# One rotating pool of eight PSUM banks instead of two pools of four, in a transformer forward pass on one core

## The chip, the cores and the metric

The kernel runs on one core of one Trainium2 chip. The metric is the device time of one execution in microseconds. Five engines work beside each other, each in its own order: TensorE (PE: matmuls, and the weight loads, PEld), VectorE (DVE), ScalarE (ACT), GpSimd (POOL) and SyncE (SP), which issues nearly all loads and stores. PE writes its results into PSUM, a memory of eight banks; a bank takes 128 partitions by 512 fp32 numbers. DVE and ACT read results out of it.

## What is computed

A batch of one, 1024 tokens of width 1024, fp32, through two blocks of two layers each. The first block's layers take one wide projection of the normalised input and feed two mixers beside each other; the second block has one gMLP layer and one chunk-attention layer.

```python
for layer in range(DEPTH):                      # first block, twice
    proj = rms_norm(x, norm_w[layer]) @ w_in[layer]
    (q, k, v, z_attn, q_h, f_h, i_h, g_h, gate_attn, gate_hgrn) = jnp.split(proj, split_points, axis=-1)
    q, k = partial_rope(q), partial_rope(k)     # 8 heads of 64, 2 key heads
    a = sliding_window_attention(q, k, v, attn_sinks[layer]) * jax.nn.silu(z_attn)
    b = norm(hgrn2_recurrence(q_h, k_h, i_h, logf)) * jax.nn.silu(g_h)
    merged = sigmoid(gate_attn) * (a @ w_up_attn[layer]) + sigmoid(gate_hgrn) * (b @ w_up_hgrn[layer])
    x = x + merged @ w_out[layer]
x = rms_norm(x, final_norm_w)
# second block
u, v, z = jnp.split(rms_norm_2(x, a_norm_g) @ a_w_in, 3, axis=-1)
x = x + (gelu(u) * (w_s @ layer_norm(gelu(v)) + b_s) * silu(z)) @ a_w_out
k, v = jnp.split(rms_norm_2(x, g_kv) @ w_kv, 2, axis=-1)
q, z = jnp.split(rms_norm_2(x, b_norm_g) @ w_qz, 2, axis=-1)
o = softmax(q @ k.T + rel_bias, over the own and the 8 earlier chunks of 64) @ v
x = x + (o * silu(z)) @ w_out
out = rms_norm_2(x, final_norm_g)
```

## The kernel before

**Products.** Every large product is done in about fp32 precision by three matmuls: each operand is split into a high and a low float32r part, and hi·hi, hi·lo and lo·hi are added in one PSUM bank. Weights come from DRAM as raw tiles of 128x1024 (fetch_w, L218 issues the load on SP), are split by a cast (ACT or DVE) and a subtraction (DVE or POOL) into wh and wl, and are used by one of three loops: unit (L259 to L261, output channels by 512 tokens), unit_tok (L272 to L274, tokens by 256 channels) and unit_wide (L286 to L288, tokens by 512 channels, two banks at once). The bank that such a product adds up in comes from Net.mm (L143); the 512 tokens of a half, or a quarter of them at the very start, are handled as a whole. All elementwise work goes through Engine.call, so that all of it is recorded at L77 whatever it does; the trace tells such instructions apart by their tiles (hp are tiles of the common heap).

**Everything else that PE does** takes its bank from Net.aux (L146): the sums of squares over the channels (a matmul with a matrix of ones: load_first L1143 at the start, mean_bcast L363 for the norms, out_last L1007 at the end), the transposes and scores of the sliding attention (swa_kv_fiber L553 for the keys, whose split is in tiles khl; swa_q_fiber L594 for the queries, L614 for the scores, L642 and L667 behind the softmax), the recurrence (hgrn_half L683 to L800), the gMLP's bias (gmlp_bias: L1214 sums, ACT copies the sum, L1219 spreads it; L1274 mixes) and the chunk attention (attn2's block: scores L1413 into aux, DVE adds the bias and reduces to the maximum in one instruction, which writes the scores to sP and the maximum to a2m; exp on ACT, scaling on POOL; transposes L1446 into aux, copied to pT; products with the values L1456).

**half_banks** (L149) gives the two heads of a block (e = 0 and e = 1) the two 256-column halves of one aux bank where their scores, or their transposes, are no wider than 256 columns; otherwise each takes a bank.

**The order of the work** is set in two steps. The program issues units of weights one after the other, and between them, each time that 24 matmuls' worth of product work has passed (tick), advances the open fibers (the attention's and the recurrence's steps, the norms' late parts) by one step. Behind that a scheduler writes each engine's order, from the dependences and from when it reckons that an instruction's operands and its bank are free. In the kernel before, a tile from mm waits for the fourth product tile ahead of it to be read out, and a tile from aux for the fourth aux tile ahead of it.

Of the kernel before, what the change touches and what calls it, by code (L numbers as in the profile page):

```python
# [9 lines left out]
F32 = mybir.dt.float32  # L10
# [9 lines left out]
P = 128  # L20
H = 512
# [76 lines left out]
class Net:  # L98
# [42 lines left out]
        return self.heap(F32R), self.heap(F32R)  # L141

    def mm(self):  # L143
        return self.ps.tile([P, H], F32, tag="mm", bufs=4, name=self.name("mm"))

    def aux(self):  # L146
        return self.ps.tile([P, H], F32, tag="aux", bufs=4, name=self.name("aux"))

    def half_banks(self):  # L149

# [1550 lines left out]
```

## Time and profile before

| | |
|---|---|
| time of three runs | 3031.61, 3034.82, 3035.86 us (median 3034.82) |
| the profiled execution's own time | 3037.59 us |
| its span in the trace | 3035.8 us |
| mean granted clock of TensorE | 0.990 |
| busy PE, PEld | 2944.6, 2444.6 us |
| busy DVE, ACT, POOL | 1767.0, 1472.9, 1162.0 us |
| matmuls and other PE instructions | 15996 |

The span is the stretch from the first to the last instruction of the profiled execution; what of its own time lies outside is 1.8 us. Busy time counts the time in which an engine executes something. The idle time before an instruction is put down to the engine and tile whose end released it; the tiles' names are those of the program with their numbers left out.

### The profile page before, as it was taken

The numbers are of one execution on the slowest core, as the hardware profiler recorded it, in microseconds if no ns is written. First come the engines' busy times: TensorE is split into PE (matmuls) and PEld (weight loads), VectorE is DVE, ScalarE is ACT, GpSimd is POOL, SyncE is SP. The second block draws the span as 40 slices with busy tenths as digits, with TensorE's granted clock in tenths as the row PEclk, the third lists the DMA queues.
The fourth block names the chain that finished last, engine by engine and source line by source line (L and its number), as shares of the span: only waits on it lengthen the run. The fifth ranks groups of instructions, "written<-read, shape, count | busy, mean of one in ns | idle before, by whom it ended". The sixth has DMA issues, their size and how long they took to land.

```text
span 3035.8 us, 43390 instructions
## 1 busy us (share of the span) xinstructions
PE 2944.6 (97%) x15996; PEld 2444.6 (81%) x15996; DVE 1767.0 (58%) x3376; ACT 1472.9 (49%) x2966; POOL 1162.0 (38%) x1217
## 2 busy tenths in 40 slices
PE   6999999999999999999999999999998999999997
PEld 6887888888878888788878888888887787878777
DVE  6557755566665666665666434454345655555566
ACT  4665336642366424674244554335544546455552
POOL 4445433543435434454332333223333434333331
PEclk9999999999999999999999999999999999999999
DMA  3212242122521224322243223433243101111123
GB/s 119 78 63 101 87 139 84 68 73 90 174 84 63 77 91 139 109 72 70 91 139 125 104 100 123 133 115 116 104 146 105 58 31 54 45 54 38 62 102 108
DMA packets 101493, 283.44 MB, mean 93 GB/s; under 512 B 11289, under 2 KB 15513, under 8 KB 101281
## 3 DMA queue, kind: packets, MB, share of 16 engines
q1 hardware_dynamic: 100016, 279.51, 27.0%
q8 instruction: 126, 2.06, 0.3%
q10 hardware_dynamic: 1264, 1.17, 0.1%
q14 instruction: 87, 0.70, 0.1%
HBM read 259.66 MB, written 20.97 MB: 92 GB/s over the span
## 4 chain that ended last, share of the span: by engine, by line
PE 86%; DVE 7%; issue 2%; ACT 2%; POOL 1%; DMA 1%; SPq 0%; DVEq 0%; POOLq 0%; ACTq 0%
PE mm L259 20%; PE mm L260 20%; PE mm L261 19%; DVE hp L77 5%; PE mm L288 3%; PE mm L286 3%; PE mm L287 3%; PE aux L683 2%; PE aux L1413 2%; PE aux L1456 1%; PE aux L1446 1%; PE mm L273 1%; PE mm L274 1%; PE mm L272 1%; PE aux L614 1%
## 5 line engine op out<-in xcount | busy, mean ns | idle before, releaser
L259 PE MATMUL mm<-hp,wh 128*128 128x512 f32 (+1 forms) x2816 | 1107.8, 393 | 1.9 <-DVE hp L77 1.9
L260 PE MATMUL mm<-hp,wh 128*128 128x512 f32 (+1 forms) x2816 | 1095.6, 389 | 0.5 <-POOL hp L77 0.5
L261 PE MATMUL mm<-hp,wl 128*128 128x512 f32 (+1 forms) x2816 | 1095.0, 389 | 0.0
L77 POOL TENSOR_TENSOR wl<-raw,wh 128x512 fp32r<-128x512 f32 x381 | 513.5, 1350 | 771.7 <-ACT wh L77 667.2
L77 POOL TENSOR_TENSOR hp<-hp,hp 128x256 f32<-128x256 f32 (+4 forms) x378 | 430.3, 1143 | 688.9 <-DVE hp L77 270.6
L77 ACT CAST wh<-raw 128x512 fp32r<-128x512 f32 x569 | 350.8, 620 | 676.8 <-PE mm L260 464.8
L259 PEld LDWEIGHTS mm<-hp,wh 128*128 128x128 f32 x2816 | 532.0, 189 | 108.1 <-issue 3.1
L261 PEld LDWEIGHTS mm<-hp,wl 128*128 128x128 f32 x2816 | 531.8, 189 | 108.3
L260 PEld LDWEIGHTS mm<-hp,wh 128*128 128x128 f32 x2816 | 532.6, 189 | 105.5 <-issue 2.6
L77 DVE TENSOR_TENSOR wl<-raw,wh 128x512 fp32r<-128x512 f32 x435 | 356.6, 822 | 215.1 <-ACT wh L77 172.8
L77 DVE TENSOR_TENSOR hp<-hp,hp 128x512 fp32r<-128x512 f32 (+3 forms) x472 | 368.3, 788 | 157.8 <-ACT hp L77 110.7
L77 ACT ACT_TABLE_LOAD x244 | 313.1, 1283 | 34.4 <-PE mm L261 15.4
L77 ACT CAST hp<-hp 128x512 fp32r<-128x512 f32 (+2 forms) x254 | 146.0, 583 | 233.8 <-POOL hp L77 183.9
L77 DVE CAST wh<-raw 128x512 fp32r<-128x512 f32 x247 | 132.3, 536 | 194.9 <-PE mm L260 165.0
L77 ACT ACTIVATE hp<-mm 128x512 f32<-128x512 f32 (+1 forms) x304 | 171.1, 574 | 152.6 <-PE mm L288 74.8
L77 DVE TENSOR_TENSOR hp<-mm,hp 128x512 f32<-128x512 f32 (+1 forms) x248 | 155.3, 633 | 144.6 <-ACT hp L77 58.8
L286 PE MATMUL mm<-wh,hp 128*128 128x512 f32 x480 | 188.2, 392 | 0.0
L287 PE MATMUL mm<-wl,hp 128*128 128x512 f32 x480 | 187.5, 391 | 0.0
L288 PE MATMUL mm<-wh,hp 128*128 128x512 f32 x480 | 187.3, 390 | 0.0
L77 POOL TENSOR_SCALAR sP<-sP,a2l 128x640 f32<-128x640 f32 (+4 forms) x128 | 88.8, 698 | 230.3 <-DVE a2l L77 181.6
L272 PE MATMUL mm<-wh,hp 128*128 128x256 f32 x448 | 129.5, 289 | 7.2 <-ACT hp L77 7.2
L77 ACT ACTIVATE sP<-sP,a2nm 128x640 f32<-128x640 f32 (+4 forms) x128 | 88.4, 691 | 96.8 <-DVE a2nm L77 95.7
(183 smaller groups left out, 3472.9 us busy)
## 6 DMA issues: line engine op xcount, KB each, us to landing
raw<-in_w_ch_dram SPq DMA_DIRECT2D x128, 512.0 KB, 3.3
raw<-in_g_uz_dram SPq DMA_DIRECT2D x64, 512.0 KB, 3.2
hp<-xd SPq DMA_DIRECT2D x88, 256.0 KB, 4.3
raw<-in_w_up_dram SPq DMA_DIRECT2D x64, 256.0 KB, 2.7
raw<-in_w_o_dram SPq DMA_DIRECT2D x32, 512.0 KB, 3.3
raw<-in_g_v_dram SPq DMA_DIRECT2D x32, 512.0 KB, 4.3
raw<-in_g_o_dram SPq DMA_DIRECT2D x32, 512.0 KB, 3.8
raw<-in_w_wide_dram SPq DMA_DIRECT2D x28, 512.0 KB, 4.0
```

The lines of the kernel that those rows point to most:

```text
L77: self.last = f(*args, **kw)
L259: nc.tensor.matmul(ps, wh[:, c : c + P], rh, start=(k == 0), stop=False)
L260: nc.tensor.matmul(ps, wh[:, c : c + P], rl, start=False, stop=False)
L261: nc.tensor.matmul(ps, wl[:, c : c + P], rh, start=False, stop=(k == nk - 1))
L272: nc.tensor.matmul(ps, lh[:, o : o + P], wh[:, c : c + n], start=(k == 0), stop=False)
L273: nc.tensor.matmul(ps, lh[:, o : o + P], wl[:, c : c + n], start=False, stop=False)
L274: nc.tensor.matmul(ps, ll[:, o : o + P], wh[:, c : c + n], start=False, stop=(k == KD - 1))
L286: nc.tensor.matmul(ps, lh[:, s], wh, start=(k == 0), stop=False)
L287: nc.tensor.matmul(ps, lh[:, s], wl, start=False, stop=False)
L288: nc.tensor.matmul(ps, ll[:, s], wh, start=False, stop=(k == KD - 1))
L683: nc.tensor.matmul(ps[:, s], k[:, s], q[:, s], start=True, stop=True)
L1413: nc.tensor.matmul(ps[:, 0:w], st[p, kk][e][half][:, o : o + P], st[p, "k"][e][hf][:, k0 : k0 + w], start=(j == 0), stop=(j == 1),)
```

## The change

The two helpers that hand out PSUM banks name one tag instead of two, so that all eight banks form one rotation:

```diff
--- before.py
+++ after.py
@@ -141,10 +141,10 @@
         return self.heap(F32R), self.heap(F32R)
 
     def mm(self):
-        return self.ps.tile([P, H], F32, tag="mm", bufs=4, name=self.name("mm"))
+        return self.ps.tile([P, H], F32, tag="bank", bufs=8, name=self.name("mm"))
 
     def aux(self):
-        return self.ps.tile([P, H], F32, tag="aux", bufs=4, name=self.name("aux"))
+        return self.ps.tile([P, H], F32, tag="bank", bufs=8, name=self.name("aux"))
 
     def half_banks(self):
```

A tile of either kind now waits for the eighth tile ahead of it, of whichever kind, to be read out. Nothing else in the program text changes; the same instructions are issued on every engine. The scheduler, which reckons with the new waits, writes another order: it differs on PE in some 800 rows, on DVE and ACT in some 250 each, on POOL in 71 and on SP in 20. In the rows below, a name's last number counts the program's tiles; + and - stand for the order now and before.

PE, from its first instructions on (L1143 sums squares of a quarter of the input; mm_299, mm_332 and mm_359 are the first products; 49 of their matmuls lie between the first and the last row):

```order
 L1143 MATMUL aux18_132<-hp14_121,ones_f_91 128x256 x2
+L1143 MATMUL aux49_209<-hp45_198,ones_f_91 128x256 x2
 L272 MATMUL mm92_299<-wh21_142,hp29_159 128x256
 L273 MATMUL mm92_299<-wl22_143,hp29_159 128x256
...
 L274 MATMUL mm99_332<-wh27_154,hp44_195 128x256
 L272 MATMUL mm100_359<-wh53_221,hp29_159 128x256
-L1143 MATMUL aux49_209<-hp45_198,ones_f_91 128x256 x2
 L273 MATMUL mm100_359<-wl54_222,hp29_159 128x256
```

The second quarter's squares moved from behind 49 matmuls to ahead of them.

PE at the norm behind the first half of the first block's second layer (L363 sums squares; mm2368 and mm2376 are products of 128x256 for the second half's tokens):

```order
 L274 MATMUL mm2368_11270<-wh2311_11111,hp2289_11014 128x256
+L363 MATMUL aux2369_11297<-hp2317_11149,ones_d_83 128x512
 L272 MATMUL mm2376_11319<-wh2304_11097,hp2241_10834 128x256
...
 L274 MATMUL mm2376_11319<-wh2311_11111,hp2287_11009 128x256
-L363 MATMUL aux2369_11297<-hp2317_11149,ones_d_83 128x512
 L272 MATMUL mm2376_11319<-wh2311_11111,hp2288_11013 128x256
```

The sum now stands straight behind mm2368, ahead of 21 matmuls of mm2376 that it stood behind.

PE in the chunk attention (scores L1413 of a block into aux4424, transposes L1446 of an earlier block, mm4436 a product):

```order
 L1446 MATMUL aux4417_21350<-ident_76,sP4375_21160 128x128
-L259 MATMUL mm4436_21413<-hp4105_19829,wh4337_20948 128x512
 L1413 MATMUL aux4424_21372<-hp4231_20521,hp4295_20810 128x256
 L1413 MATMUL aux4424_21372<-hp4231_20521,hp4296_20811 128x256
...
 L1413 MATMUL aux4429_21388<-hp4320_20901,hp4297_20816 128x512
 L1413 MATMUL aux4429_21388<-hp4320_20901,hp4298_20817 128x512
+L259 MATMUL mm4436_21413<-hp4105_19829,wh4337_20948 128x512
 L260 MATMUL mm4436_21413<-hp4106_19830,wh4337_20948 128x512
```

One product that stood ahead of a block's scores now stands behind the first of them; the second half of that bank comes after it as before.

## Rows read from the trace of the kernel before

**Rows 1.** The page: totals by engine, and the chain that ended last by engine.

```profile
PE 2944.6 (97%) x15996; PEld 2444.6 (81%) x15996; DVE 1767.0 (58%) x3376; ACT 1472.9 (49%) x2966; POOL 1162.0 (38%) x1217
...
PE 86%; DVE 7%; issue 2%; ACT 2%; POOL 1%; DMA 1%; SPq 0%; DVEq 0%; POOLq 0%; ACTq 0%
```

**Rows 2.** Busy time by stretch: its length, engines' busy us (instructions), granted clock, DMA.

```profile
2280.00:2356.00 76.00, 66.11 (x329) 56.65 (x329) 45.62 (x71) 40.10 (x98) 29.70 (x22) 0.93 0.29 102
2356.00:2432.00 76.00, 69.37 (x445) 56.79 (x443) 51.22 (x129) 42.44 (x116) 35.85 (x38) 0.98 0.17 56
```

**Rows 3.** What PE waited for over the span (total us, times, longest).

```profile
PE aux L1413 <- DVE a2m L77: 18.8, 11, 8.9
PE aux L1413 <- DVE pT L77: 11.2, 11, 2.5
...
PE aux L1446 <- DVE pT L77: 4.0, 5, 2.1
...
PE aux L1413 <- ACT hp L77: 2.0, 3, 1.4
```

**Rows 4.** Timeline at 2411 us: start, duration, engine, line, operation [idle before].

```profile
2410.47 0.68 DVE L77 COPY pT<-aux 128x512 f32<-128x512 f32 x1
...
2411.17 1.39 DVE L77 TENSOR_TENSOR hp<-hp,hp 64x512 fp32r<-64x512 f32 x2
...
2411.20 1.43 PE L1413 MATMUL aux<-hp,hp 128*128 128x256 f32 x6 [2.46 <-DVE pT L77]
...
2413.20 0.29 DVE L77 CUSTOM_DVE_ANT_0 sP<-aux,bias 128x128 f32<-128x128 f32 x1
...
2413.55 0.50 PE L1413 MATMUL aux<-hp,hp 128*128 128x256 f32 x2
```

**Rows 5.** Busy time by stretch at the start.

```profile
18.10:28.40 10.30, 9.21 (x49) 8.31 (x49) 8.38 (x13) 6.98 (x16) 6.29 (x7) 1.00 0.15 51
55.80:66.20 10.40, 4.63 (x19) 3.38 (x20) 5.67 (x12) 4.50 (x21) 9.17 (x33) 0.60 0.12 46
```

**Rows 6.** PE's timeline at the start.

```profile
28.48 0.48 PE L1143 MATMUL aux<-hp,ones_f 128*128 128x256 f32 x1 [1.04 <-DVE hp L77]
```

**Rows 7.** PE's timeline around 466 us.

```profile
465.38 0.46 PE L594 MATMUL aux<-identr,hp 128*128 128x128 f32 x4
...
466.21 0.39 PE L288 MATMUL mm<-wh,hp 128*128 128x512 f32 x1
466.44 0.40 PE L286 MATMUL mm<-wh,hp 128*128 128x512 f32 x1
466.74 0.74 PE L614 MATMUL aux<-hp,hp 128*128 128x256 f32 x4
```

**Rows 8.** PE's timeline around 1202 us.

```profile
1202.47 0.47 PE L363 MATMUL aux<-hp,ones_d 128*128 128x512 f32 x1 [2.81 <-DVE hp L77]
```

**Rows 9.** ACT's timeline around 1219 us.

```profile
1218.22 0.90 ACT L77 CAST khl<-hp 128x128 fp32r<-128x128 f32 x4 [3.31 <-PE aux L553]
1219.03 0.65 ACT L77 ACTIVATE hp<-mm 128x256 f32<-128x256 f32 x2
1219.56 1.31 ACT L77 CAST hp<-aux 128x128 fp32r<-128x128 f32 x6
```

**Rows 10.** PE's timeline around 1725 us.

```profile
1724.63 0.50 PE L260 MATMUL mm<-hp,wh 128*128 128x512 f32 x1
...
1725.76 1.15 PE L1219 MATMUL aux<-hp,hp 2*128 2x128 f32 x8
```

**Rows 11.** PE's timeline in the tail.

```profile
3000.32 1.13 PE L1007 MATMUL aux<-hp,ones_f 128*128 128x256 f32 x4
...
3015.69 0.39 PE L259 MATMUL mm<-hp,wh 128*128 128x256 f32 x1 [1.89 <-DVE hp L77]
```

**Rows 12.** The chain of waits in the tail (start, us, what).

```profile
3017.16 0.12 PE mm L260
...
3020.44 0.21 PE mm L261
```

## The prediction

> **What bounds the kernel now.** The page's totals come first: TensorE (PE) is busy 2944.6 of 3035.8 us, no other engine comes near, and the chain that ended last runs on PE for 86% [rows 1]. No bank rotation can shorten 2944.6 us of products; the change can only fill, move or lengthen the remaining 91.2 us (3035.8 − 2944.6) in which PE stands idle, and the stretches behind them at TensorE's lower clock level (1.2 instead of 2.4 GHz). So the second view is busy time by stretches: the attention of the second block is where idle time is spread widest, 69.37 busy of 76 us in one slice [rows 2]. The third is the list of what PE waited for [rows 3]: its longest entries are the scores (L1413) and the transposes (L1446) of that attention, behind VectorE (DVE). The fourth is the timeline at each place where PE's order changes.
>
> **What kind of wait it is.** A PE wait at a new bank can mean two things: the bank is still being read for an older tile, which a larger pool may cure, or the other half of the same tile is still being read, which it can't. In the list, waits on a pT or hp copy are of the first kind or of the nearly related second head of a transpose bank: 11.2 + 4.0 + 2.0 = 17.2 us. Waits on a2m are of the second kind: the two heads of a block share a bank, and the second head's scores wait until DVE has reduced the first's. They are the largest entry, 18.8 us, 8.9 of it in one piece [rows 3]. The change leaves half_banks as it is, so all 18.8 stay.
>
> The 17.2 us are the upper bound of the attention's gain. I take 4, because of what stands behind such a wait [rows 4]. At 2411.20 PE had waited 2.46 us for a DVE copy; with a free bank these first-half scores run at about 2408.7. But the second half of the tile waits for DVE's reduction of the first, and DVE works down its own queue in order: the copy of 2410.47, then a 1.39 us split, another copy, and only at 2413.20 the reduction, so the second half runs at 2413.55 in either order. PE has the same few products (five before, of which one moves behind the scores) to put between. The idle time moves a few rows on. What is gained is where DVE had nothing queued in between: I put 4 of 17.2 us; the lower end is −1, for blocks in which a filler moved the wrong way.
>
> The Trainium skill ("Perfetto Trace Analysis", Identifying Performance Opportunities) says that the same gap repeating on the engine that should be saturated can mean that PSUM has no room for the next tile. By that rule all 17.2 us would go, and the sum below would be 13.2 us lower; it is the first rival's reading. The rows agree for the pT entry and disagree for the larger a2m entry, which is one of the reasons for 4.
>
> **Part by part: what moves.** The edit adds and removes no instruction. The scheduler, seeing other bank releases, writes another order on every engine, and mostly it places an aux product as soon as a bank exists, ahead of products that used to cover its wait.
>
> *Start.* The squares of the second quarter (L1143) move from behind 49 products to ahead of them. They wait for DVE's sum and ran at 28.48 after a 1.04 us idle [rows 6]. In the new order PE has nothing to do until then, and the 9.21 us of busy time between 18.1 and 28.4 come after. The reserve that takes them up is the stretch 55.8 to 66.2, where PE waited for the key splits (khl) and was busy 4.63 of 10.40 us: 5.8 us idle [rows 5]. 9.2 − 5.8 = 3.4 us longer. Ends: 0 (the half clock there, 0.60, would also shrink) and 9.2 (in the new order all sixteen key transposes stand ahead of the 48 products that were strewn between them, and two weight splits are put into POOL's rope chain ahead of khl, so the wait may shift by as much). I take **+3.4**.
>
> *Fillers ahead of L614 and L553.* A 128x512 product comes every 0.23 us (466.21 to 466.44) [rows 7]. The four products before L614 at 466.74 cover ScalarE's (ACT's) copy of the transposed query, whose L594 began at 465.38 [rows 7]; in the new order they stand behind L614, at three such places. At eight other L614 places one product moves likewise, and at two L553 places two: 12 + 8 + 4 = 24 products, 5.5 us. Ends 0 (a later wait takes them in) and 5.5; PE is busy 97% of the span [rows 1] and so has few later waits, so **+4.5**.
>
> *Second norm.* L363 ran after 21 products of the next tile and then still waited 2.81 us, until 1202.47, for DVE's split of its operand [rows 8], whose chain hangs on other products, not on these 21. Now it stands ahead of them: at 0.12 us a product [rows 12], 2.5 us of cover go, and the wait grows to 5.3 us. Ends 0 (waits further on take the products in) and 3.8 (half clock behind the longer gap adds 1.3, as in the tail below). **+2.5**.
>
> *Key splits in layer two.* ACT's four khl casts came at 1218.22, ahead of the activations and evacuation copies of 1219.03 and 1219.56; now two more activations (0.65 us together) and twelve such copies (1.31 for six) stand before them [rows 9]: 3.3 us later. POOL's subtraction and PE's next transposes hang on them, with no product between. Ends 0 and 3.3; **+2.5**.
>
> *gMLP bias.* At four groups, L1214 is followed by an ACT copy and L1219; four products ran between, from 1724.63 until L1219 at 1725.76 [rows 10], 1.13 us. They move behind L1219. The copy's length stays, so about 0.75 of it turns idle, four times: **+3.0**, ends 0 and 4.5.
>
> *Tail.* L1007 ran at 3000.32 right as DVE's sum was ready, behind 41 products [rows 11]; it now stands ahead of them at 2995.3 and waits 5.0 us. In return the wait for a product bank at 3015.69, 1.89 us, goes with its half clock (0.21 instead of 0.12 a product, 16 of them up to 3020.44: 1.4) [rows 11, 12]. I assume the same half-clock cost of 1.4 behind the new gap: 5.0 − 3.3 + 1.4 = **+3.1**. Ends 0 and 6.5: SyncE also puts the residual's load (L993) behind two output stores, and DVE's read of the old bank waited for such a load.
>
> **Sum.** 3.4 + 4.5 + 2.5 + 2.5 + 3.0 + 3.1 − 4.0 = +15.0 us. Against the profiled execution: span 3035.8 to 3050.8, its own time 3037.59 to 3052.6. That execution lies 2.8 us over the median of the runs shown, 3034.82; on the median, 3049.8, so **3050 us**. A measurement of this kernel can tell about 0.2% (6.1 us) from no change, so "same" is 3028.8 to 3040.9.
>
> **Rivals.**
> A. *The waits for banks really go* and PE runs ahead: 17.2 us of them vanish, and the displaced fillers, gMLP products and casts are only done later in gaps that exist anyway. Left are start, norm and tail, 9.0: 9.0 − 17.2 = −8.2, 3027 us, faster. It decides where DVE's queue is empty when a free bank lets the scores start early. For it: the 11.2 us entry is the second largest. Against: DVE's unbroken row around 2411. Chance 0.14.
> B. *Losses absorbed.* Gain 4 as forecast, but only norm and tail (5.6) cost something, as later waits at khl, L614 and L1219 end at times that other engines set anyway: about +2, 3037 us, same. For it: L614 at 466.74 shows no wait at all [rows 7]. Against: it shows none because the fillers were there. Chance 0.24.
> C. *More short gaps lower the clock.* After each longer gap PE ran at half clock (0.21 a product [rows 12]); the slice with the 8.9 us wait has a mean granted clock of 0.93, the next 0.98 [rows 2]. If the moved waits pulled the 608 us of attention (2356 to 2964) from 0.98 to 0.93, that is 608 × (0.98/0.93 − 1) = 33 us, with the sum 3082 us. The Trainium skill ("TensorE: Matmul & The Clock Gate", A second HAM failure mode: psum-queue depth-cycling) tells of a kernel that cycled through PSUM banks, idled shortly between groups and had its clock swing. No row here shows that a rotation by itself does so: with one of four banks products follow each other at 0.23 us [rows 7]. Chance 0.04.
> The forecast itself: 0.58, from 3041 to 3062 by its own ends.
>
> **Numbers.** Below 3028.8 only A lies: 0.14 faster. B is 0.24 same. Forecast and C are 0.62 slower. The range leaves out C and A's lower tail: 3026 to 3062, where 3062 has the start at about 9 and the tail at 6.5 with the others as taken.
>
> **What would show it.** Right: an L1143 wait near 20 us ending at about 28.5; an L363 wait of some 5 us near 1200 with a DVE releaser; L1219 and L614 as new entries of 2 to 4 us each in PE's list; an L1007 wait of 5 us in the tail and no product wait behind it; a2m still near 18.8, and larger by what the pT entry loses. Wrong: pT entries gone with a2m unchanged (A), or the new waits there but later ones shorter by as much (B), or a mean clock in the attention slices under 0.95 (C).

## The result, and the profile after

The changed kernel takes 3056.38 us (median of four runs, 3053.34 to 3064.2) against 3034.21 before (four runs): a ratio of 1.0075 with a 95% interval of 1.0063 to 1.0088, 22 us slower. The forecast was slower, 3050 in a range of 3026 to 3062. In the profiled executions the span grew from 3035.8 to 3055.8 us, by 20.0. The page of the changed kernel:

```profile
span 3055.8 us, 43358 instructions
...
PE 2938.9 (96%) x15996; PEld 2449.1 (80%) x15996; DVE 1755.1 (57%) x3376; ACT 1474.5 (48%) x2966; POOL 1161.5 (38%) x1217
...
PE 86%; DVE 8%; ACT 2%; issue 2%; POOL 1%; DMA 1%; SPq 0%; DVEq 0%; POOLq 0%; ACTq 0%
```

PE's busy time fell by 5.7 us [rows 1], so its idle time grew by 25.7, from 91.2 to 116.9 (3055.8 − 2938.9). Where, the list of what PE waited for says (total us, times, longest):

```profile
PE aux L1413 <- DVE a2m L77: 35.0, 22, 8.9
PE aux L1143 <- DVE hp L77: 25.5, 2, 17.4
PE aux L363 <- DVE hp L77: 10.6, 5, 4.9
PE aux L553 <- POOL khl L77: 7.3, 5, 3.0
PE aux L1446 <- DVE pT L77: 6.0, 5, 2.3
PE aux L1007 <- DVE hp L77: 4.8, 1, 4.8
PE aux L614 <- ACT hp L77: 4.4, 11, 0.9
PE aux L1219 <- ACT hp L77: 3.1, 4, 1.1
PE aux L553 <- ACT khl L77: 2.2, 1, 2.2
```

Beside [rows 3], the kernel before had these entries at the same places, and none at L614 and L1219:

```profile
PE aux L1143 <- DVE hp L77: 10.0, 2, 8.9
PE aux L363 <- DVE hp L77: 9.4, 5, 4.7
PE mm L272 <- ACT hp L77: 7.2, 1, 7.2
...
PE aux L553 <- POOL khl L77: 3.5, 7, 1.6
...
PE aux L1007 <- DVE hp L77: 0.9, 1, 0.9
```

Three things differ. The pT entry of L1413, 11.2 us, is gone, and so is the hp entry; a2m grew from 18.8 to 35.0, and the pT entry of L1446 from 4.0 to 6.0. L614, L1219 and the 4.8 us at L1007 are new or have grown from tenths. At the start, the first products' wait of 7.2 us (L272) now lies within a longer one of L1143. No wait of a product for a bank has come in. The timeline of PE shows the places (start, duration, operation, idle before):

```profile
27.62 2.07 PE L1143 MATMUL aux<-hp,ones_f 128*128 128x256 f32 x4 [17.39 <-DVE hp L77]
29.13 0.78 PE L272 MATMUL mm<-wh,hp 128*128 128x256 f32 x1
...
1205.50 0.50 PE L363 MATMUL aux<-hp,ones_d 128*128 128x512 f32 x1 [3.91 <-DVE hp L77]
...
1227.66 0.28 PE L553 MATMUL aux<-identr,khl 128*128 128x128 f32 x1 [2.20 <-ACT khl L77]
1230.96 0.91 PE L553 MATMUL aux<-identr,khl 128*128 128x128 f32 x4 [3.02 <-POOL khl L77]
...
1740.30 1.15 PE L1219 MATMUL aux<-hp,hp 2*128 2x128 f32 x8 [0.67 <-ACT hp L77]
...
1743.23 0.63 PE L260 MATMUL mm<-hp,wh 128*128 128x512 f32 x1
1743.66 0.63 PE L261 MATMUL mm<-hp,wl 128*128 128x512 f32 x1
...
2427.38 1.41 PE L1413 MATMUL aux<-hp,hp 128*128 128x256 f32 x6
...
2431.41 0.50 PE L1413 MATMUL aux<-hp,hp 128*128 128x256 f32 x2 [1.48 <-DVE a2m L77]
...
3017.87 2.08 PE L1007 MATMUL aux<-hp,ones_f 128*128 128x256 f32 x4 [4.84 <-DVE hp L77]
...
3019.96 0.41 PE L260 MATMUL mm<-hp,hp 128*128 128x256 f32 x1
```

The squares of the second quarter wait 17.39 us from 10.2 on, in place of 7.2 and 1.0 before [rows 6], and the first product starts at 29.13. L363 waits with DVE as its releaser [rows 8], L553 twice. At 2427.38, the place that answers to [rows 4], the scores start without a wait, and 2.5 us later their second half waits 1.48 us for a2m. L1007 waits 4.84 us [rows 11], and the product behind it comes at half clock.

How late PE is at each of these places can be read from the first or last matmul of a line, in the view of one line. The same table gives the experiments of the next section, as the difference to before in us; where a kernel's program is the same as before up to a place, as x4, x5 and x7 are before the attention, the differences of −3.3 to +1.4 show how far one execution scatters. x7's execution shown is its fastest, 6 us under its median.

| matmul of | before | changed | x1 | x3 | x4 | x5 | x6 | x7 |
|---|---|---|---|---|---|---|---|---|
| L286, first | 73.3 | +1.7 | +2.7 | +0.6 | −1.2 | −0.9 | +2.2 | −1.5 |
| L800, last before 1150 us | 1081.8 | +4.4 | +10.2 | +3.1 | −0.5 | −1.0 | +5.1 | −0.7 |
| L614, last | 1340.0 | +14.3 | +20.6 | +12.8 | −0.1 | +1.1 | +15.1 | −0.6 |
| L1214, first | 1674.6 | +12.5 | +19.5 | +12.7 | 0.0 | +1.1 | +13.2 | −3.3 |
| L1219, last | 1825.9 | +17.5 | +21.6 | +14.7 | +1.2 | +1.4 | +17.9 | −2.7 |
| L1456, last | 2952.2 | +17.5 | +35.3 | −16.5 | −1.7 | +0.7 | +16.7 | −35.9 |
| L1007, last | 3024.9 | +20.3 | +39.6 | −12.0 | −2.1 | +4.1 | +17.5 | −31.5 |

In the changed kernel the loss is made before the attention, 17.5 us by 1826; through the 1126 us that follow, the attention among them, nothing is lost or won; the tail adds 2.8.

### The profile page after: what moved, and what is told of

It reads as the page before. It is cut to its first block, busy times and chain, and to the rows that moved or that the text cites. A ratio compares the mean times of both kernels' runs of the same rounds, so it can differ in the third digit from the quotient of the medians.

```text
span 3055.8 us, 43358 instructions
## 1 busy us (share of the span) xinstructions
PE 2938.9 (96%) x15996; PEld 2449.1 (80%) x15996; DVE 1755.1 (57%) x3376; ACT 1474.5 (48%) x2966; POOL 1161.5 (38%) x1217
## 4 chain that ended last, share of the span: by engine, by line
PE 86%; DVE 8%; ACT 2%; issue 2%; POOL 1%; DMA 1%; SPq 0%; DVEq 0%; POOLq 0%; ACTq 0%
PE mm L259 20%; PE mm L260 20%; PE mm L261 20%; DVE hp L77 5%; PE mm L286 3%; PE mm L287 3%; PE mm L288 3%; PE aux L683 2%; PE aux L1456 1%; PE aux L1413 1%; PE aux L1446 1%; PE mm L272 1%; PE mm L274 1%; PE mm L273 1%; PE aux L614 1%
## 5 line engine op out<-in xcount | busy, mean ns | idle before, releaser
L286 PE MATMUL mm<-wh,hp 128*128 128x512 f32 x480 | 188.1, 392 | 0.0
L272 PE MATMUL mm<-wh,hp 128*128 128x256 f32 x448 | 129.0, 288 | 0.0
```

What stands on the lines that cost most here:

```text
L272: nc.tensor.matmul(ps, lh[:, o : o + P], wh[:, c : c + n], start=(k == 0), stop=False)
L286: nc.tensor.matmul(ps, lh[:, s], wh, start=(k == 0), stop=False)
```

## The experiments

**The theories.** O: the loss is the order. Numbers of tiles in the orders count where the program first writes them. Before, 98 of 1250 bank tiles are first written behind a tile that the program writes later, 97 of them aux tiles behind a product; in the changed kernel none is. Tiles of one tag take their banks in the program's order, so with one tag a product can no longer run ahead of an aux bank that the program fills earlier, however many banks are free; that takes the cover from the waits. S: the loss is the shared banks themselves, products and aux waiting for each other's readers. Two further pairs concern the attention and stand with their runs.

**x1: two pools of four, with the order of one pool.** Edges on PE alone, which cost no wait, hold each bank's first matmul behind that of the bank before it in the program:

```diff
+def in_program_order(tc):
+    dep = mybir.DependencyInfo(mybir.DependencyClass.NoSync, mybir.DependencyReason.DATA)
+    seen, prev = set(), None
+    for i in list(tc.nc.cur_bb.bb.instructions):
+        if i.engine == mybir.EngineType.PE and i.outs:
+            tile_name = i.outs[0].bass_ap.tensor.name
+            if tile_name not in seen:
+                seen.add(tile_name)
+                if prev is not None:
+                    tc.add_manual_dep(i, prev.name, dep, reason="program order")
+                prev = i
...
         Net(ctx, tc, a, out).run(stop)
+        in_program_order(tc)
```

> The kernel before with its two pools of four banks; added are only edges on PE that let no bank's first matmul run ahead of the first matmul of a bank that the program hands out earlier, as one rotation does by itself. Theory O (the loss is this order: products can't be placed ahead of an earlier aux bank): 3050 to 3060 us, 16 to 26 over before; an L1143 wait near 17 us, L1219 and L614 waits of 3 to 4 us, an L1007 wait near 5 us, as in the changed kernel. Rival S (the loss is the shared eight banks, products and aux waiting for each other's readers): 3031 to 3039 us, as before, since products keep banks of their own.

Measured: 3076.06 us (3074.98 to 3080.6), a ratio of 1.0132, interval 1.0115 to 1.0149, to 3035.06 before. Its list of PE's waits:

```profile
PE aux L1143 <- DVE hp L77: 25.7, 2, 17.4
PE aux L1413 <- DVE a2m L77: 20.5, 12, 9.2
PE aux L1413 <- DVE pT L77: 12.3, 11, 3.3
...
PE aux L1007 <- DVE hp L77: 4.8, 1, 4.8
...
PE aux L614 <- ACT hp L77: 4.4, 11, 0.9
...
PE aux L1219 <- ACT hp L77: 3.1, 4, 1.1
```

Products kept four banks of their own, and the loss is there all the same, with the changed kernel's waits at L1143, L614, L1219 and L1007 to a tenth or so. S falls. O is right on the kind of the loss and too low on its size, 41 us instead of 16 to 26: the a2m and pT waits stand beside each other, and the table shows another 13.7 us lost in the attention (35.3 − 21.6), where the changed kernel loses none. So the change has two parts: the order, which costs some 41 us while the banks stay four and four, and eight banks instead, which give back some 20 of them (3076 − 3056), most of it in the attention.

**x2: products that take their bank early.** In the changed kernel mm() handed out a tile made one (two) products earlier:

```diff
     def mm(self):
-        return self.ps.tile([P, H], F32, tag="bank", bufs=8, name=self.name("mm"))
+        return bank_ahead(self, lambda: self.ps.tile([P, H], F32, tag="bank", bufs=8, name=self.name("mm")))
...
+def bank_ahead(net, make):
+    if not hasattr(net, "ahead"):
+        net.ahead = [make() for _ in range(BANKS_AHEAD)]
+    net.ahead.append(make())
+    return net.ahead.pop(0)
```

> The changed kernel, eight banks in one rotation, but a product takes its bank one product earlier in the program, so that it may run ahead of aux banks handed out since; one bank of eight stands reserved. Theory O: a good part of the loss comes back, 3036 to 3046 us; the L1219 and L1007 waits go. Rival S: as the changed kernel or worse, 3053 to 3065, since one bank fewer rotates.

> The same with two products ahead, two of eight banks reserved. Theory O: most of the loss comes back, 3030 to 3040 us, the L1143 wait below 12 us. Rival S: 3055 to 3070, worse than one ahead.

Measured: 3059.85 and 3055.82 us (ratios 1.0074 and 1.0070). O's number was missed, but the edit did nothing: PE's matmuls (14488 in the program) stand in the changed kernel's order, line by line: a tile made earlier keeps its place as long as it is first written where it was. The two runs tell nothing between O and S; they repeat the changed kernel's time.

**x5 and x6: one pool in one stage only.** The PSUM pool is closed and opened again where the chunk attention begins: in x5 two pools of four up to there and one of eight from there (its edit is shown), in x6 the other way round:

```diff
+def psum_pool(net, name, one):
+    net.ps_ctx = net.ctx.enter_context(ExitStack())
+    net.ps = net.ps_ctx.enter_context(net.tc.tile_pool(name=name, bufs=1, space=PSUM))
+
+    def bank(kind):
+        return net.ps.tile([P, H], F32, tag="bank" if one else kind, bufs=8 if one else 4, name=net.name(kind))
+
+    net.bank = bank
...
             self.next_small_pool("small2")
+            self.ps_ctx.close()
+            psum_pool(self, "psum2", one=True)
```

> Two pools of four up to the chunk attention, there closed and replaced by one rotation of eight for the attention and the tail. Theory O (the loss is the order outside the attention, where few banks are short; inside, the order's loss and the banks' gain cancel): 3035 to 3042 us. Rival S (the loss is where banks are short, in the attention): 3048 to 3058 us.

> The mirror image: one rotation of eight up to the chunk attention, two pools of four from there on. Theory O: 3047 to 3056 us, with L1143, L553, L614 and L1219 waits as in the changed kernel and L1413's as in the kernel before. Rival S: 3033 to 3040 us.

Measured: x5 3038.38 us, ratio 1.0010 (0.9999 to 1.0020); x6 3060.66, ratio 1.0075 (1.0060 to 1.0090). x6 is a little above O's range, but no further from before than the changed kernel is. The whole loss is made before the attention, where the list shows no product that waits for a bank. In x5 the a2m entry is 33.9 us against 18.8 before, and the time does not move: the pT waits have turned into a2m waits.

**x8 and x9: the order at a few places.** Two pools of four, and edges as in x1, but products are held only behind the banks of the norms and the gMLP's bias (x8), or only behind those of the first attention's keys, queries and scores (x9):

```diff
+HELD_BY = ('mean_bcast', 'gmlp_bias')
...
+                if tile_name.startswith("mm") and holder is not None:
+                    tc.add_manual_dep(i, holder.name, dep, reason="held")
+                elif tile_name.startswith("aux") and int(tile_name[3:].split("_")[0]) in HOLDERS:
+                    holder = i
```

> The kernel before with its two pools of four; products handed out later are held behind the first matmul of a norm's (L363) or the gMLP bias's (L1214, L1219) bank alone. Theory O: the norm's place near 1202 us costs 2 to 4 us, the wait at L363 growing to about 5, and the four bias places 0.7 to 1.7 us each, with L1219 waits of about 3 us in all; 3037 to 3046 us. Rival S: under 1 us in all.

> The same, products held behind the first attention's key transposes and query and score banks (L553 to L667) alone. Theory O: 3 to 4 us by 1190 us through L614 waits, then 5 to 7 us at the key transposes near 1220 us; 3042 to 3050 us, with L614 waits near 4.4 us and L553 waits on khl near 10. If the 1220 us place needs the norm's delay ahead of it: only 0 to 3 us there.

Measured, in one execution each, so without an interval: x8 3057.75 us, x9 3046.12, before 3037.66 (median of nine). x9 lies in its range, x8 12 us above its own. Between the last L800 and the last L614 x8 loses 10.9 us (from −2.1 to +8.8), the changed kernel 9.9 and x9 only 2.7 (+5.1 to +7.8). The waits of PE from 1190 to 1260 us, in x8:

```profile
PE aux L363 <- DVE hp L77: 6.3, 1, 6.3
PE aux L553 <- POOL khl L77: 3.4, 1, 3.4
```

and in x9:

```profile
PE aux L363 <- DVE hp L77: 2.6, 1, 2.6
PE aux L614 <- ACT hp L77: 1.2, 2, 1.0
PE aux L553 <- POOL khl L77: 0.8, 2, 0.5
```

So the key transposes' delay near 1220 us comes with the norm's place, not with the keys' own. x8's expectation was for 2 to 4 us there and too low; S, with under 1 us, is out. At the bias x8 lost more than expected too: its L1219 waits sum to 3.1 us, as expected, but the time from the first L1214 to the last L1219 grew by 4.9 us (8.5 to 13.4). Another 6 us came behind it (+19.6 at the last L1007), at places that I have not followed up. The loss up to 1082 us is x9's: its L614 waits sum to 4.5 us, as expected, and it is 5.1 us late there, while x8 is not late at all.

**x10: two sums later in the program.** The changed kernel, with the bias's L1219 (here L1221) called from zwork, behind the next product, and a second yield ahead of norm_two's first mean_bcast:

```diff
-        ps = self.aux()
-        for i in range(4):
...
+        def spread():
+            ps = self.aux()
+            for i in range(4):
...
         def zwork(hd, ps):
+            if half == 0 and hd % 4 == 0:
+                st["bias"] = st["spread"]()
+                nc.sync.dma_start(out=self.gd[hd // 4], in_=st["bias"])
...
             yield
+            yield
             rstd = self.rstd_of(self.mean_bcast(m[0], self.ones_d))
```

> The changed kernel, with two sums traced later in the program: the gMLP bias's L1219 behind the next product instead of before it, and the second norm's L363 one step of 24 products later. Theory O: the L1219 waits go, the L363 wait near 1200 us shrinks by 2 to 5 us, and the time falls to 3044 to 3052 us. Rival S (the order of the program is not what costs): 3053 to 3060 us.

Measured: 3048.54 us (3044.99 to 3056.64), a ratio of 1.0043 (1.0026 to 1.0060) to 3037.66. Against the changed kernel, each by its own ratio, that is about 10 us won back (0.0032 of 3035) with two edits of the program's order and the same one pool. The L1219 entry is gone, and L363's fell from 10.6 to 6.7:

```profile
PE aux L363 <- DVE hp L77: 6.7, 4, 4.9
```

The a2m entry (here L1418) stands at 35.6, and the wait of L553 for POOL near 1220 us at 3.3, though no L363 waits there any more. O holds; the program's order is what one rotation turns into PE's order.

**x3, x4 and x7: whole banks in the attention.** The a2m waits are for the second half of a bank by theory W; by its rival Q, DVE's queue would hold PE up whatever the bank. The edit gives each head a bank of its own, with eight banks (x3), with four and four (x4), and with the pools of x5 (x7):

```diff
         def take():
-            if not rest:
-                ps = self.aux()
-                rest.extend([ps[:, 256:512], ps[:, 0:256]])
-            return rest.pop()
+            ps = self.aux()
+            return ps[:, 0:256]
```

> The changed kernel, but each head's scores and transposes of up to 256 columns take a bank of their own instead of half of a shared one. Theory W (the a2m waits of 35.0 us are for the other half of the same bank): the a2m entry falls below 15 us, and the time to 3035 to 3048 us. Rival Q (DVE's queue in order sets the pace there, whatever the bank): the wait moves to pT, sP or another copy, and the time stays within 5 us of 3056.

> The kernel before, two pools of four, but each head's scores and transposes of up to 256 columns take a bank of their own. Theory E (whole banks pay only where eight banks rotate, since each block then needs up to two banks more): 3025 to 3045 us, with the waits on pT copies above the 11.2 us of before. Rival F (the shared halves alone cost the time, whatever the number of banks): 3003 to 3015 us, a2m under 12 and pT no larger.

> Two pools of four up to the chunk attention, from there one rotation of eight with a whole bank for each head. If the two effects add (no loss before the attention; inside it the gain that the changed kernel with whole banks had): 3003 to 3016 us, faster than both kernels by 20 to 30 us. If whole banks gained by what the new order had put behind before the attention, not by themselves: 3022 to 3035 us.

Measured: x3 3030.25 us, ratio 0.9977 (0.9966 to 0.9987) to before; x4 3034.42, ratio 0.9993 (0.9983 to 1.0002); x7 3012.19 (3005.93 to 3012.76), ratio 0.9918 (0.9902 to 0.9935), 25 us faster than before and 44 faster than the changed kernel. x4's waits, where the halves' wait has only changed its name, which fits four aux banks being too few:

```profile
PE aux L1413 <- DVE pT L77: 24.0, 22, 2.6
PE mm L259 <- ACT hp L77: 12.0, 2, 10.0
```

And x7's from 2330 to 2910 us, where no a2m and hardly a pT is left:

```profile
PE mm L259 <- ACT raw L77: 7.2, 1, 7.2
...
PE aux L1413 <- ACT hp L77: 3.7, 4, 1.2
PE mm L259 <- DVE pT L77: 3.3, 1, 3.3
```

The 7.2 us were there before under another name. They end at 2347.56, at the opening of the attention, where scores waited 8.9 us for a2m, the longest wait of [rows 3]; in the kernel before DVE works there through a row of other instructions and reduces only behind it:

```profile
2338.19 10.87 DVE L77 TENSOR_TENSOR hp<-hp,hp 128x512 f32<-128x512 f32 x9
...
2348.98 0.28 DVE L77 CUSTOM_DVE_ANT_0 sP<-aux,bias 128x128 f32<-128x128 f32 x1
```

So 8.9 us of the a2m entries hang on DVE's queue, as Q says, and with whole banks PE still stands idle there (7.4 us in x3, 10.0 in x4); the rest, 9.9 us before and 26.1 in the changed kernel, is what they cure.

The busy time from 2356 to 2964 us (us of each engine, then the granted clock) in the kernel before:

```profile
2356.00:2964.00 608.00, 579.75 (x3757) 472.92 (x3756) 358.03 (x1025) 323.22 (x787) 233.29 (x252) 0.99 0.16 55
```

in the changed kernel:

```profile
2356.00:2964.00 608.00, 566.09 (x3710) 467.44 (x3709) 361.31 (x1040) 330.12 (x807) 241.81 (x258) 0.98 0.16 53
```

and in x7:

```profile
2356.00:2964.00 608.00, 586.80 (x3951) 499.39 (x3950) 380.32 (x1051) 328.50 (x807) 243.69 (x255) 0.99 0.18 59
```

The stretch is the same in time, not in work, since the kernels are shifted against each other; PE is busy for 580, 566 and 587 of its 608 us. W holds, and Q falls but for that one wait at the opening: with whole banks and eight of them DVE's queue did not hold PE up behind it. x3 gained even more than W said (26 us to the changed kernel, 8 to 21 expected). F falls with x4: whole banks alone pay nothing. E's mechanism is as said: the pT wait grew, to 24.0 us. The Trainium skill's rule that a gap which repeats can mean too little PSUM ("Perfetto Trace Analysis", Identifying Performance Opportunities) fits these runs if both halves are done: eight banks, and no two heads in one; x5 and x4, with one half each, gained nothing.

## Why the prediction was right, and where it was off

The direction and the range held, and by the reason given: aux work is placed ahead of products that used to cover its wait. The sum was +15.0 us, the profiled execution +20.0. (The range's upper end, 3062, adds its terms to the profiled execution's 3052.6; from 3049.8, where the forecast stands, they give 3059. The measured 3056.38 is below both.) Term by term, from the table:

| term | forecast | measured |
|---|---|---|
| start | +3.4 | +1.7 |
| fillers (to 1082 us) | +4.5 | +2.7 |
| second norm and key splits (1082 to 1340 us) | +5.0 | +9.9 |
| 1340 to 1675 us | 0 | −1.8 |
| gMLP bias | +3.0 | +5.0 |
| attention | −4.0 | 0.0 |
| tail, with what follows it | +3.1 | +2.5 |

*Start, fillers, tail* came as described: a 17.4 us wait that ends at 27.62, an L614 entry of 11 waits (8 + 3 places were named) and 4.4 us, an L1007 wait of 4.8 us with half clock behind it. The sizes were within 2 us, which is no finer than one execution tells.

*Norm and key splits* is the term that was mis-sized, 5.0 against 9.9. I priced two parts, 2.5 of lost cover and 2.5 of ACT's queue, and left two at nothing: POOL's order behind ACT, and the clock behind the key waits (behind the norm's it stood only in the upper end). L363's wait grew by 1.1 us (2.81 to 3.91), not by 2.5. ACT's order is as I read it, the key casts behind activations and ten copies:

```profile
1224.17 1.34 ACT L77 ACTIVATE hp<-mm 128x256 f32<-128x256 f32 x4 [4.02 <-PE mm L288]
1225.40 2.02 ACT L77 CAST hp<-aux 128x128 fp32r<-128x128 f32 x10
1227.18 1.00 ACT L77 CAST khl<-hp 128x128 fp32r<-128x128 f32 x4
```

They account for the 2.20 us that L553 waits at 1227.66. The 3.02 us at 1230.96 are POOL's. In the kernel before, POOL subtracted the keys' split first and rotated two query tiles (128x64; a key tile's rotation is 128x32) behind it:

```profile
1218.60 2.15 POOL L77 TENSOR_TENSOR khl<-hp,khl 128x128 fp32r<-128x128 f32 x4 [3.47 <-ACT khl L77]
1220.71 0.77 POOL L77 TENSOR_TENSOR ropea<-hp,cos 128x64 f32<-128x64 f32 x1
```

In the changed kernel the query tiles stand ahead, and the keys wait for them:

```profile
1224.64 0.75 POOL L77 TENSOR_TENSOR ropea<-hp,cos 128x64 f32<-128x64 f32 x1 [7.25 <-ACT hp L77]
...
1230.46 1.70 POOL L77 TENSOR_TENSOR khl<-hp,khl 128x128 fp32r<-128x128 f32 x4
```

POOL has the new order in x1, x8 and x10 too, and the old one in x9, where the norm keeps its place; x8 shows that the norm's place is enough to bring it about. Why the scheduler then turns POOL's order round stays open. The clock is the other half. From 1190 to 1260 us (the columns as above), before and in the changed kernel:

```profile
1190.00:1260.00 70.00, 66.33 (x365) 55.72 (x364) 50.79 (x88) 36.75 (x104) 35.17 (x49) 1.00 0.35 121
```

```profile
1190.00:1260.00 70.00, 59.74 (x308) 51.09 (x307) 44.70 (x77) 32.36 (x87) 25.99 (x43) 0.93 0.30 106
```

PE's waits in these 70 us grew from 3.6 to 10.2 us, and a granted clock of 0.93 instead of 1.00 is worth some 4.9 us more by my estimate (70 × 0.07); the 9.9 us are a little less than the two together. In x8, which lost 10.9, the clock was 0.88; in x9, which lost 2.7, 0.98.

*gMLP bias.* The waits are 3.1 us, as forecast, 3.0. What the 5.0 has beyond them is mostly clock, which I had given no price there: behind two of the four places products come 0.43 us apart, as from 1743.23 to 1743.66, against 0.23 at full clock [rows 7], seven of them behind 1689 and some five here, some 2 us in all. That part is a matter of the single execution: with the same waits of 3.1 us, x1 and x3 lost 2.1 and 2.0 us there, at a clock of 1.00 from 1675 to 1850 us, where the changed kernel's is 0.98.

*Attention.* The argument was right and my 4 us were not: of the 17.2 us, the pT and hp entries of L1413 (11.2 + 2.0) went and that of L1446 grew by 2.0, a2m grew by 16.2, and the last L1456 is as late as the last L1219. The idle time moved to the second half of the bank completely. One reading was wrong, though it did not change the sum: not all 18.8 us of a2m were for the other half, 8.9 of them were the opening wait behind DVE's queue. The sign to look for that I had named, a2m "larger by what the pT entry loses", is what came.

*Rivals.* A: the waits for other tiles' banks did go, with nothing won, so A fell at the point it named, the wait behind. B fell: norm and keys, fillers and bias were not absorbed, 17.5 us by 1826. C fell: the mean clock of the span is 0.988 against 0.990, that of the attention 0.98 against 0.99. Its premise, half clock after each longer gap, was more than the rows show: behind the 2.81 us wait at 1202.47 [rows 8] the products of the kernel before came 0.12 us apart. But where it looked for nothing, around the norm and the keys, the clock is half of the loss.

*From 1340 to 1675 us* the 1.8 us are scatter: the kernel before had a clock of 0.94 between 1580 and 1610, the changed kernel 1.00, and so had x7, which has the program of the kernel before up to the attention and won 2.7 us here.

*Left open*: what the order costs within the attention on its own. x1 has 13.7 us there, with four aux banks, and I have no run with eight banks and the old order. Each edit of the banks also lets the scheduler write a new order, so x3 and x7 show what whole banks and the order that comes with them are worth together.

## What to carry to other kernels

A pool's tag is also a queue: what shares it takes its buffers in the program's order, so merging two pools that serve long work and short dependent work forbids the long work to run ahead of short work that the program writes earlier, and the cover of many small waits goes. Before widening a pool, see from the wait list whether the engine waits for an older tile, for the other half of the same one, or for a reader that is itself held up in its queue; here eight banks paid only where the halves were given up too, and only in the stage that was short of banks (x7, 25 us). Prices of moved work should follow the data behind it to the end, here from a moved norm to the order in which ACT and POOL serve the keys, and allow for the clock behind each new gap.

## What was not expected of the hardware

TensorE's granted clock was at its lower level (0.50, 1.2 instead of 2.4 GHz) behind short gaps as well, though not behind each. After L1219's wait of 0.67 us at 1740.30, itself between small matmuls, it was 0.50 from 1742.0 to 1745.3 and the products came 0.43 us apart, while at the same work before, without the wait, it was 1.00 (1725 to 1732). At the two later bias places, with waits of 0.66 us, it stayed at 1.00 (1791 to 1797 and 1841 to 1847). In x8 it was the second and the fourth place where it fell, and in x1, with the same four waits, none (1.00 from 1675 to 1850 us). A 3.91 us wait at L363 left products 0.21 us apart instead of 0.12 until 1209.3, while 2.81 us there before left them at 0.12. So with the same waits the loss at the bias differed by 3 us between these executions, and the time lost at a place can exceed the waits listed there.
